# Norming the first two tiles' columns: diagonals behind each root, VectorE instead of GpSimd, and tiles 2 and 3 in a written order

## The chip, the core and the metric

The kernel runs on one core of a Trainium2 chip. A core has TensorE (PE, matrix products into PSUM), VectorE (DVE), ScalarE (ACT), GpSimd (POOL) and SyncE (SP, here only a queue for DMAs). Each engine runs its own instructions in order and waits for others by semaphores. The metric is device time in microseconds (us) of one execution; a smaller time is better.

## What is computed

The kernel is one block of a streaming encoder for 1024 tokens of width 1024, all in float32. Only the first lines of it matter here: the input is normed, and projected by a wide matrix.

```python
def rmsnorm(x, g):
    y = x * lax.rsqrt(jnp.mean(x * x, axis=-1, keepdims=True) + RMS_EPS)
    return y * g

h = rmsnorm(x, norm_mix_pre)                       # 1024 x 1024
proj = jnp.einsum("bsd,dn->bsn", h, w_in)          # q, k, v, f_logit, convolution, gates
...                                                # conv branch, forgetting attention, merge
x = x + rmsnorm(m, norm_mix_post)
x = x + rmsnorm(swiglu(rmsnorm(x, norm_ffn_pre)), norm_ffn_post)
```

## The kernel before

The tokens are cut into eight tiles of 128 rows. For each tile the kernel needs the normed rows transposed (columns of 128 tokens, so that the width lies on the partitions), and it needs them three times over: as a pair of reduced-precision numbers `hB..h` and `hB..l` (high part and rest, made by `split`: ACT copies the high part, DVE subtracts it), and, for the tiles 0 to 3, as full numbers in `hraw`. A product of two such pairs is three passes on PE: high by high (`hh`), high by low (`hl`), low by high (`lh`). The projections that follow use Strassen's scheme, and `hT12` and `hT34` are the sums and differences that it needs. While the columns come in, PE already makes `v` and the forget logits of each tile: `pv`, 8 slices of the width x 3 passes x 2 halves = 48 products a tile, by the weights `wvh` and `wvl`. ACT takes `pv` to `vs`, POOL issues its store to `v_dram`, and DVE adds a bias to the last columns (`ff`).

Tiles 0 and 1 (class `First`) are transposed as they are, before their norm is known: DVE scales the columns by the gain (`hraw`, then the split), the products go ahead, and the token's root (1/norm) is multiplied in when ACT takes `pv` to `vs`. A root is made by `root`: POOL adds epsilon to the sum of squares (`va`) and takes the power -1/2 (`r`). The columns in `hraw` still lack this root, and it differs from column to column. So two diagonal matrices are made from `ident` and the roots, a product with a matrix of ones (`rp`) puts each root in all 128 rows, the columns are multiplied by it, and they are split anew.

Tiles 2 to 7 are normed first: ACT squares and sums (`norm_sum`), POOL makes the root, DVE multiplies (`norm_rest`, which also issues the load of the tile three further on), PE transposes (`turn`, giving `tp`, four banks in turn), and both halves are split. `turn` gives back a function `rest`, called later by hand: for the tiles 2 and 3 it copies `tp` to `hraw`, for the later ones it makes the Strassen sums.

The order: up to the product `rp` all engines keep the order in which the code is written; this is what `steps_` and its row of short names are for (`wh3`: ACT's high part of weight slice 3, `wl1`: DVE's rest of slice 1, `s11`: DVE's scaling of the second half of tile 1, `h11` and `l11`: its split, `x11`: its transposes, `phl01`: PE's pass `hl` of slice 1 for tile 0, `sq` and `pw`: squares and roots). From there on a scheduler decides within a stage where `strict[0]` does not name the engine. Before, tile 2's `rest` was under a written order of DVE, ACT and POOL, and the loop over the tiles from 2 on was free. Every element operation goes through a helper at line 76, so the profile shows one line for all; the names of the tiles tell them apart.

Of the kernel before, what the change touches and what calls it, by code (L numbers as in the profile page):

```python
# [10 lines left out]
F32 = mybir.dt.float32  # L11
F32R = mybir.dt.float32r
AF = mybir.ActivationFunctionType
ALU = mybir.AluOpType
# [3 lines left out]
P = 128  # L18
# [3 lines left out]
ST = S // P  # L22
# [24 lines left out]
def block_kernel(  # L47
# [18 lines left out]
    strict = [()]  # L66

    class InOrder:
# [15 lines left out]
    nc = SimpleNamespace(  # L84
        **{e: InOrder(e) for e in engines}
    )
# [7 lines left out]
    def pool(name, bufs=1, side="left", space=None):  # L94
        kw = dict(name=name, bufs=bufs)
        if space is not DRAM:
            kw["reuse_waits"] = "tile"
        if space is not None:
            kw["space"] = space
        else:  # L100
            kw["side"] = side
        stack = ExitStack()
        ctx.callback(stack.close)
        return stack.enter_context(tc.tile_pool(**kw)), stack.close

    def f32(ap):
        return ap.bitcast(F32)

    def add(o, a, b):
        nc.vector.tensor_tensor(o, a, b, op=ALU.add)  # L110

    def sub(o, a, b):
        nc.vector.tensor_tensor(o, a, b, op=ALU.subtract)

    def mul(o, a, b):
        nc.vector.tensor_tensor(o, a, b, op=ALU.mult)

    def copy(o, a):
        nc.scalar.activation(o, a, AF.Copy)

    def split(hi, lo, src):

        copy(hi, src)
        sub(lo, src, f32(hi))
# [32 lines left out]
    ident = cpool.tile([P, P], F32, name="ident")  # L157
# [19 lines left out]
    def st_tile(name, w=1):  # L177
        return stat.tile([P, w], F32, tag=name, name=name)

    def rms_scale(ms, plus=EPS, tile_=st_tile, w=1, between=None):  # L180

        va = ms
        if plus is not None:
            va = tile_("va", w)
            nc.gpsimd.tensor_scalar(va, ms, plus, None, op0=ALU.add)
        r1 = tile_("r1", w)
        nc.gpsimd.tensor_tensor(r1, va, power[:, :w], op=ALU.pow)
        if between:
            between()
        return r1  # L190
# [7 lines left out]
    def z_tile(name, dt=F32, w=S):  # L198
        return zp.tile([P, S], dt, tag="z", name=name, bufs=2)[:, :w]

    h_pool, h_close = pool("h1", side="right")
    def h_pair(name, shape):
        return [h_pool.tile(shape, F32R, name=f"{name}{t}") for t in "hl"]

    hB11 = h_pair("hB11", [P, 4, NC])
    hT12 = h_pair("hT12", [P, 2, 4, NC])
    hB21 = h_pair("hB21", [P, 4, NC])
# [4 lines left out]
    av, av_close = pool("av")  # L212
    psa, psa_close = pool("psa", 4, space=PSUM)

    def load_x(st, between=None):
        xt = ax.tile([P, D], F32, tag="x", name="xt", bufs=3)
        rows = x2d[st * P : (st + 1) * P, :]
        for c in (n1, n2) if between else (slice(0, D),):
            nc.sync.dma_start(xt[:, c], rows[:, c])
            if between and c is n1:  # L220
                between()
        return xt
# [31 lines left out]
    def vs_tile():  # L254
        return av.tile([P, VF], F32, tag="vs", name="vs", bufs=2)
# [5 lines left out]
    def flat_(t):  # L261
        return t.rearrange("p a b -> p (a b)")
# [22 lines left out]
    def norm_sum(st):  # L285

        xt = xq.pop(st)
        hn = ap.tile([P, D], F32, tag="hn", name="hn", bufs=2)
        ssq = st_tile("ssq")
        nc.scalar.activation(hn, xt, AF.Square, scale=ROOT, accum_out=ssq)  # L290
        return xt, hn, ssq

    def norm_rest(st, xt, hn, rs):

        nc.vector.scalar_tensor_tensor(hn, xt, rs, gm, op0=ALU.mult, op1=ALU.mult)
        if st + 3 < ST:
            xq[st + 3] = load_x(st + 3)
        return hn
# [5 lines left out]
    def turned(hn, q):  # L304

        tp = psa.tile([P, 4, P], F32, tag="mm", name="tp")
        for k in range(4):
            kt = 4 * q + k
            nc.tensor.transpose(tp[:, k, :], hn[:, kt * P : (kt + 1) * P], ident)
        return tp  # L310

    hraw = av.tile([P, KT, NC], F32, name="hraw")

    class First:
# [10 lines left out]
        def turn(self, q):  # L325
            self.tps[q] = turned(self.xt, q)
# [17 lines left out]
        def root(self):  # L344
            self.rs = rms_scale(self.ssq)
# [59 lines left out]
    def v_tile(st, ops):  # L405
        pv = psa.tile([P, 2, NC], F32, tag="pv", name="pv", bufs=2)
        for k in range(KT):
            src = ops[k // 4]
            for n in range(2):
                cs = slice(n * hv, (n + 1) * hv)  # L410
                mm3(
                    pv[:, n, :hv],
                    (src[0][:, k % 4, :], src[1][:, k % 4, :]),
                    (wvh[:, k, cs], wvl[:, k, cs]),
                    k == 0,
                    k == KT - 1,
                )
        v_out(st, pv)
# [3 lines left out]
    def v_out(st, pv, **kw):  # L422
        vs = vs_tile()
        nc.scalar.activation(
            vs.rearrange("p (n c) -> p n c", n=2), pv[:, :, :hv], AF.Copy, **kw
        )
        nc.gpsimd.dma_start(v_dram[st * P : (st + 1) * P, :], vs[:, :AW])
        flast.append((st, vs))
        if st:
            for t, x in flast:  # L430
                add(ff[:, t, :], x[:, AW:VF], bf)
            flast.clear()


    firsts = [First(t) for t in range(2)]
    later, norms = {}, {}

    def square(t):
        if t < 2:
# [8 lines left out]

    def root(t):
        if t < 2:  # L450
            firsts[t].root()
            if t == 0:
                nc.gpsimd.dma_start(bf, b_f[0].partition_broadcast(P))
        else:
            norms[t] = rms_scale(later[t][2])
# [13 lines left out]
    def steps_(row):  # L469
# [7 lines left out]
    parts = [Parts(f.ops) for f in firsts]  # L477
    steps_(
# [5 lines left out]
    )  # L484
    hn = norm_rest(2, *later[2][:2], norms[2])
    steps_("plh06 pw3 phh16 plh16 phl05 phl15 phh07")
    hn3 = norm_rest(3, *later[3][:2], norms[3])
    steps_("pw1")
    cur = turn(2, hn)
    hn = hn3  # L490
    steps_("plh07 phl06 phl07")
    v_out(0, parts[0].pv, scale=firsts[0].rs)
    steps_("phh17 plh17 phl16 phl17")
    v_out(1, parts[1].pv, scale=firsts[1].rs)
    z = z_tile("rs")
    dg = z[:, : 2 * P].rearrange("p (t c) -> p t c", t=2)
    rb = z[:, 2 * P : 4 * P]
    for t, f in enumerate(firsts):
        nc.gpsimd.tensor_scalar(dg[:, t, :], ident, f.rs, None, op0=ALU.mult)
    rp = psa.tile([P, 4, P], F32, tag="mm", name="rp")[:, :2, :]  # L500
    nc.tensor.matmul(flat_(rp), ones, flat_(dg), start=True, stop=True)
    copy(rb, flat_(rp))
    both = slice(0, 2 * P)

    def raw_both(q):
        return hraw[:, 4 * q : 4 * q + 4, both]

    for q in range(2):
        nc.gpsimd.tensor_tensor(
            raw_both(q), raw_both(q), rb.unsqueeze(1).broadcast_to([P, 4, 2 * P]),  # L510
            op=ALU.mult,
        )
    strict[0] = ("vector", "scalar", "gpsimd")
    cur[1]()

    def settle():

        for q, (hh, hl) in enumerate((hB11, hB21)):
            split(hh[:, :, both], hl[:, :, both], raw_both(q))

    strict[0] = ()
    for st in range(2, ST):
        ops, rest = cur
        if st + 1 < ST:
            cur = turn(st + 1, hn)
        if st + 2 < ST:
            hn = norm(st + 2)
        if st + 3 == ST:
            ax_close()
            w0, w0_close = pool("w0", side="right")  # L530

            def w0_tile(tag, dt=F32R):
                return w0.tile([P, KT, P], dt, tag=tag, name=tag, bufs=1)

            r0, h0, l0 = w0_tile("r0", F32), w0_tile("h0"), w0_tile("l0")
            nc.sync.dma_start(r0, win[:, C_Q : C_Q + P].rearrange("(k p) m -> p k m", p=P))
            split(h0, l0, r0)
        if st > 2:
            v_tile(st, ops)
            rest()  # L540
        else:
            v2 = Parts(ops)
            for q in range(2):
                for what in ("hh", "hl", "lh"):
                    v2.run(what, *range(4 * q, 4 * q + 4))
            v_out(2, v2.pv)
            settle()

    av_close()
    ap_close()  # L550
# [557 lines left out]
    for ij, (kind, j, _, _) in enumerate(jobs):  # L1108
# [4 lines left out]
        if ij < 2:  # L1113
            if ij == 0:
# [6 lines left out]
                firsts = []  # L1121
# [52 lines left out]
        elif kind == "gb":  # L1174
            for m, parts in ((j, (c11, c12)), (j + 1, (c21, c22))):
                zt = zts.pop(m)
                for n in range(2):
# [5 lines left out]
                    for t in (1, 0):  # L1183
                        lag = 2 - t
                        c = slice(0 if n else lag, NC)
# [422 lines left out]
    for n in range(2):  # L1608
        ns = slice(n * NC, (n + 1) * NC)
        for d in range(KT):  # L1610
# [16 lines left out]
            if n == 0 and d < 4:  # L1627
                op, half = (w11, w21)[d // 2], slice(d % 2 * 2, d % 2 * 2 + 2)
# [388 lines left out]
    rest = Pairs([f_src(f) for f in range(NPRE)], prep_rest_alone)  # L2017
    whole = Pairs([f_src(f) for f in range(NPRE, NF)])
    for f in range(NF):
# [25 lines left out]
        if f == NF - 2:  # L2045
            ra, rb = pairs_of(raw_t()), pairs_of(raw_t())
# [262 lines left out]
```

## Time and profile before

| | us |
|---|---|
| three timed runs | 1319.67, 1319.72, 1321.43 (median 1319.72) |
| the profiled execution | 1321.18, of it 1319.30 in the span of the trace |
| PE busy | 1307.6 |
| DVE busy | 920.1 |
| ACT busy | 557.1 |
| POOL busy | 192.9 |

The first 65 us of the span are the stage of the tiles; from 64.75 us on the Strassen products `b` begin. A busy PE need not be at full speed: its clock is granted by a throttle, and the windows of the profile show the granted share.

### The profile page before, as it was taken

To read this page: it belongs to the slowest core of one execution; us is meant where nothing else is said; L and a number is where in the kernel's file an instruction comes from. 1 tells how busy PE (TensorE), PEld (TensorE's weight loads), DVE (VectorE), ACT (ScalarE), POOL (GpSimd) and SP (SyncE) were. 2 spreads that over 40 slices of the span, in tenths; PEclk is the share of its full clock that TensorE was granted. 3 is DMA by queue.
4 is the path that set the end of the run, shared out by engine and by line. 5 is a ranking of instruction groups with operands and counts; after the bars stand their busy time and mean duration, and the time that the engine had idled before them with its cause. 6 is when DMAs were issued, how large, how long until landed. Compare 5 with 4: busy or idle time off the path is not lost.

```text
span 1319.3 us, 17686 instructions
## 1 busy us (share of the span) xinstructions
PE 1307.6 (99%) x6695; PEld 1089.6 (83%) x6695; DVE 920.1 (70%) x1312; ACT 557.1 (42%) x868; POOL 192.9 (15%) x351
## 2 busy tenths in 40 slices
PE   8999999999999999999999999999999999999998
PEld 8988888888888888888888878888888888888886
DVE  6983768776656766676677788866766666677674
ACT  6631323344355766513678432222323234344451
POOL 4111001021112222001223112211001110000001
PEclk9999999999999999999999999999999999999999
DMA  6252423555536544674476565533323337966551
GB/s 224 78 171 88 130 71 104 185 203 188 196 138 201 156 142 161 210 252 138 135 229 227 175 193 197 177 120 104 94 90 112 112 104 271 358 224 191 159 168 64
DMA packets 168533, 215.71 MB, mean 164 GB/s; under 512 B 11496, under 2 KB 113968, under 8 KB 168448
## 3 DMA queue, kind: packets, MB, share of 16 engines
q1 hardware_dynamic: 146480, 141.39, 34.4%
q0 software_dynamic: 21952, 73.19, 15.2%
q8 instruction: 52, 0.85, 0.3%
q14 instruction: 33, 0.27, 0.1%
q10 hardware_dynamic: 16, 0.00, 0.0%
HBM read 153.41 MB, written 61.15 MB: 163 GB/s over the span
## 4 chain that ended last, share of the span: by engine, by line
PE 96%; DVE 2%; ACT 1%; issue 1%; DMA 0%; POOL 0%; DVEq 0%; POOLq 0%; ACTq 0%
PE b L76 60%; PE pd L76 16%; PE pba L76 3%; PE pbb L76 3%; PE pv L76 3%; PE po L76 2%; PE tps L76 2%; PE sp L76 2%; PE tp L76 1%; PE ma L76 1%; PE mb L76 1%; DMA raw<-in_w_gate_up_dram 0%; DVE um L76 0%; DVE c L76 0%; PE spin L76 0%
## 5 line engine op out<-in xcount | busy, mean ns | idle before, releaser
L76 DVE TENSOR_TENSOR c<-c,b 128x512 f32<-128x512 f32 x215 | 146.9, 683 | 97.5 <-PE b L76 87.5
L76 DVE TENSOR_TENSOR lo<-raw,hi 128x1024 fp32r<-128x1024 f32 (+1 forms) x91 | 109.7, 1205 | 79.7 <-PE b L76 65.6
L76 ACT ACTIVATE hi<-raw 128x1024 fp32r<-128x1024 f32 (+1 forms) x98 | 99.6, 1016 | 101.9 <-PE b L76 67.9
L76 ACT ACTIVATE hi<-sx 128x1024 fp32r<-128x1024 f32 x44 | 46.8, 1063 | 208.6 <-PE b L76 181.8
L76 DVE TENSOR_TENSOR lo<-sx,hi 128x1024 fp32r<-128x1024 f32 x44 | 53.8, 1223 | 39.2 <-PE b L76 35.8
L76 PE MATMUL b<-w12h,lo 128*128 128x512 f32 x208 | 81.0, 389 | 0.0
L76 PE MATMUL b<-w12l,hi 128*128 128x512 f32 x204 | 79.5, 390 | 0.0
L76 PE MATMUL b<-w12h,hi 128*128 128x512 f32 x204 | 79.5, 390 | 0.0
L76 PE MATMUL b<-hh,hi 128*128 128x512 f32 x176 | 69.1, 393 | 0.4 <-DVE c L76 0.4
L76 PE MATMUL b<-hl,hi 128*128 128x512 f32 x176 | 68.6, 390 | 0.0
L76 PE MATMUL b<-hh,lo 128*128 128x512 f32 x176 | 68.6, 390 | 0.0
L76 DVE TENSOR_TENSOR sx<-raw 128x512 f32<-128x512 f32 x78 | 53.7, 688 | 20.6 <-DMA raw<-in_w_in_dram 11.6
L76 PE MATMUL b<-w,s4h 128*128 128x512 f32 x208 | 64.1, 390 | 0.0
L76 PE MATMUL pd<-hi,lo 128*128 128x512 f32 x160 | 62.4, 390 | 0.0
L76 PE MATMUL pd<-hi 128*128 128x512 f32 x160 | 62.0, 390 | 0.0
L76 POOL DMA_DIRECT2D a_dramA<-um x33 | 17.9, 541 | 276.9 <-DVE um L76 276.3
L76 PE MATMUL pd<-ghi 128*128 128x512 f32 x148 | 57.7, 390 | 0.0
L76 PE MATMUL pd<-glo,ghi 128*128 128x512 f32 x148 | 57.7, 390 | 0.0
L76 PE MATMUL pd<-ghi,glo 128*128 128x512 f32 x148 | 57.6, 390 | 0.0
L76 PE MATMUL b<-hT34h,hi 128*128 128x512 f32 x136 | 53.1, 390 | 0.4 <-DVE c L76 0.4
L76 PE MATMUL b<-hT34h,lo 128*128 128x512 f32 x136 | 53.0, 390 | 0.0
L76 PE MATMUL b<-hT34l,hi 128*128 128x512 f32 x136 | 53.0, 390 | 0.0
(458 smaller groups left out, 3586.7 us busy)
## 6 DMA issues: line engine op xcount, KB each, us to landing
raw<-in_w_gate_up_dram SPq DMA_DIRECT2D x52, 512.0 KB, 3.8
raw<-in_w_in_dram SPq DMA_DIRECT2D x35, 512.0 KB, 3.9
a_dramS<-um POOLq DMA_DIRECT2D x44, 256.0 KB, 3.1
a_dramA<-um POOLq DMA_DIRECT2D x33, 256.0 KB, 2.6
sg<-sg_dram SPq DMA_DIRECT2D x32, 256.0 KB, 4.6
graw<-a_dramS SPq DMA_DIRECT2D x14, 512.0 KB, 4.3
sg_dram<-c POOLq DMA_DIRECT2D x24, 256.0 KB, 2.6
raw<-in_w_down_dram SPq DMA_DIRECT2D x11, 512.0 KB, 4.6
```

The lines of the kernel that those rows point to most:

```text
L76: ins = getattr(self.engine, name)(*args, **kw)
```

## The change

The two diagonals get a tile of their own (`dg`), and each is made on POOL directly behind its root. The product `rp` is put between the passes of tile 2. Its result is no longer copied to SBUF by ACT and multiplied by POOL: DVE multiplies `hraw` by it straight out of PSUM. Tile 2 and the turn of tile 3 no longer run in the free loop but in a written order, with the norm of tile 4 and the new splits of the tiles 0 and 1 at given places; the loop starts at tile 3. In the row of the first two tiles `s11` and `wh3` move forward.

```diff
+    dg = av.tile([P, 2, P], F32, name="dg")
 ...
     def root(t):
         if t < 2:
-            firsts[t].root()
+            f = firsts[t]
+            f.root()
+            nc.gpsimd.tensor_scalar(dg[:, t, :], ident, f.rs, None, op0=ALU.mult)
 ...
-        "phh01 wl1 plh01 z1 wh2 phh10 l10 phl10 phh11 phl01 s11 phl11 phh02 wl2 h11 plh02 phh12 "
-        "plh10 wh3 plh11 plh12 wh4 wl3 phh03 plh03 phh13 wh5 l11 plh13 phl02 wh6 phl12 wl4 "
+        "phh01 s11 plh01 z1 wl1 wh2 phh10 l10 phl10 phh11 wh3 phl01 phl11 phh02 wl2 h11 plh02 phh12 "
+        "plh10 plh11 plh12 wh4 wl3 phh03 plh03 phh13 wh5 l11 plh13 phl02 wh6 phl12 wl4 "
 ...
     cur = turn(2, hn)
-    hn = hn3
 ...
     v_out(1, parts[1].pv, scale=firsts[1].rs)
-    z = z_tile("rs")
-    dg = z[:, : 2 * P].rearrange("p (t c) -> p t c", t=2)
-    rb = z[:, 2 * P : 4 * P]
-    for t, f in enumerate(firsts):
-        nc.gpsimd.tensor_scalar(dg[:, t, :], ident, f.rs, None, op0=ALU.mult)
+    cur[1]()
+    LO_, UP_ = range(4), range(4, 8)
+    v2 = Parts(cur[0])
+    v2.run("hh", *LO_)
     rp = psa.tile([P, 4, P], F32, tag="mm", name="rp")[:, :2, :]
     nc.tensor.matmul(flat_(rp), ones, flat_(dg), start=True, stop=True)
-    copy(rb, flat_(rp))
     both = slice(0, 2 * P)
-    for q in range(2):
-        nc.gpsimd.tensor_tensor(
-            raw_both(q), raw_both(q), rb.unsqueeze(1).broadcast_to([P, 4, 2 * P]),
-            op=ALU.mult,
-        )
-    strict[0] = ("vector", "scalar", "gpsimd")
+    raws = [hraw[:, 4 * q : 4 * q + 4, both] for q in range(2)]
+    v2.run("hl", *LO_)
+    for raw in raws:
+        mul(raw, raw, flat_(rp).unsqueeze(1).broadcast_to([P, 4, 2 * P]))
+    sum4 = norm_sum(4)
+    v2.run("lh", *LO_)
+    cur = turn(3, hn3)
+    hn = norm_rest(4, *sum4[:2], rms_scale(sum4[2]))
+    for what in ("hh", "hl", "lh"):
+        v2.run(what, *UP_)
+    for (hh, hl), raw in zip((hB11, hB21), raws):
+        split(hh[:, :, both], hl[:, :, both], raw)
+    v_out(2, v2.pv)
     cur[1]()
     strict[0] = ()
-    for st in range(2, ST):
+    for st in range(3, ST):
         ops, rest = cur
 ...
-        if st > 2:
-            v_tile(st, ops)
-            rest()
-        else:
-            ...            # tile 2: the passes hh, hl, lh by halves, v_out, the splits
+        v_tile(st, ops)
+        rest()
```

The second `cur[1]()` of the new order is the `rest` of tile 3, and the loop, whose first tile is now 3, calls the same function once more.

What this does to the order on PE, from the end of tile 1's passes to those of tile 2 (`pv` with `hB11` and `hB21`; `tp` are the transposes of tile 3):

```order
 L76 MATMUL pv<-wvl,hB21h 128x260 x4
 L76 MATMUL pv<-wvh,hB11h 128x260 x8
+L76 MATMUL rp<-dg,ones 128x256
 L76 MATMUL pv<-wvl,hB11h 128x260 x8
-L76 MATMUL pv<-wvh,hB11l 128x260 x6
-L76 MATMUL rp<-rs,ones 128x256
+L76 MATMUL pv<-wvh,hB11l 128x260 x8
 L76 MATMUL tp<-ident,hn 128x128 x8
-L76 MATMUL pv<-wvh,hB11l 128x260 x2
 L76 MATMUL pv<-wvh,hB21h 128x260 x8
```

The product `rp` moves forward by 14 products, to a place behind the first eight of tile 2. At the same place on ACT (`vs` of the tiles 0 and 1, the square `hn,ssq` of tile 4, the splits of tile 3):

```order
+L76 ACTIVATE vs<-pv,r_278 128x520
+L76 ACTIVATE vs<-pv,r_414 128x520
+L76 ACTIVATE hraw<-tp 128x4x128 x2
 L76 ACTIVATE hn,ssq<-xt 128x1024
-L76 ACTIVATE vs<-pv,r_412 128x520
-L76 ACTIVATE rs<-rp 128x256
-L76 ACTIVATE hraw<-tp 128x4x128 x2
 L76 ACTIVATE hB11h<-tp 128x4x128
 L76 ACTIVATE hB21h<-tp 128x4x128
```

Tile 1's `vs` and the copies of tile 2's columns now stand ahead of tile 4's square, and the copy of `rp` is gone. On DVE, from the biases of tiles 0 and 1 to the scaling of tile 5 (`hn`):

```order
-L76 TENSOR_TENSOR ff<-vs,bf 128x8
-L76 SCALAR_TENSOR_TENSOR hn<-xt,r_479,gm 128x1024
-L76 TENSOR_TENSOR ff<-vs,bf 128x8
+L76 TENSOR_TENSOR ff<-vs,bf 128x8 x2
+L76 TENSOR_TENSOR hraw<-hraw,rp 128x4x256 x2
 L76 TENSOR_TENSOR hB11l<-tp,hB11h 128x4x128
 L76 TENSOR_TENSOR hB21l<-tp,hB21h 128x4x128
+L76 SCALAR_TENSOR_TENSOR hn<-xt,r_503,gm 128x1024
 L76 TENSOR_TENSOR hB11l<-hraw,hB11h 128x4x256
 L76 TENSOR_TENSOR hB21l<-hraw,hB21h 128x4x256
```

The scaling of tile 4 (the first `hn`) moves from ahead of tile 3's splits to behind them, and the two multiplications by `rp` stand ahead of both. On SP the loads of tiles 4 and 5 change places: tile 4's goes out first now and waits for the end of tile 1's square, where before it went out when tile 2 had been scaled.

More of the change, by code (lines that the diff above doesn't have):

```diff
@@ L494, in block_kernel @@
     v_out(1, parts[1].pv, scale=firsts[1].rs)
-    z = z_tile("rs")
-    dg = z[:, : 2 * P].rearrange("p (t c) -> p t c", t=2)
-    rb = z[:, 2 * P : 4 * P]
-    for t, f in enumerate(firsts):
-        nc.gpsimd.tensor_scalar(dg[:, t, :], ident, f.rs, None, op0=ALU.mult)
+    cur[1]()
+    LO_, UP_ = range(4), range(4, 8)
+    v2 = Parts(cur[0])
+    v2.run("hh", *LO_)
     rp = psa.tile([P, 4, P], F32, tag="mm", name="rp")[:, :2, :]
     nc.tensor.matmul(flat_(rp), ones, flat_(dg), start=True, stop=True)
-    copy(rb, flat_(rp))
     both = slice(0, 2 * P)
-    def raw_both(q):
-        return hraw[:, 4 * q : 4 * q + 4, both]
-    for q in range(2):
-        nc.gpsimd.tensor_tensor(
-            raw_both(q), raw_both(q), rb.unsqueeze(1).broadcast_to([P, 4, 2 * P]),
-            op=ALU.mult,
-        )
-    strict[0] = ("vector", "scalar", "gpsimd")
+    raws = [hraw[:, 4 * q : 4 * q + 4, both] for q in range(2)]
[11 more added lines that the diff above has]
+    v_out(2, v2.pv)
     cur[1]()
-    def settle():
-        for q, (hh, hl) in enumerate((hB11, hB21)):
-            split(hh[:, :, both], hl[:, :, both], raw_both(q))
     strict[0] = ()
-    for st in range(2, ST):
+    for st in range(3, ST):
         ops, rest = cur
@@ L537, in block_kernel @@
             split(h0, l0, r0)
-        if st > 2:
-            v_tile(st, ops)
-            rest()
-        else:
[L542 to L547, printed above, removed]
+        v_tile(st, ops)
+        rest()
     av_close()
```

## The prediction

> **What bounds the kernel now.** I read the page first, then the waits of TensorE (PE), then the windows and the timeline around the longest wait. The first line below is the page's row of busy time; the other two are the longest rows of PE's waits (who waited for whom: us in total, times, longest).
>
> ```profile
> PE 1307.6 (99%) x6695; PEld 1089.6 (83%) x6695; DVE 920.1 (70%) x1312; ACT 557.1 (42%) x868; POOL 192.9 (15%) x351
> PE rp L76 <- POOL rs L76: 2.4, 1, 2.4
> PE spin L76 <- DVE zero L76: 1.4, 1, 1.4
> ```
>
> PE is busy for 99% of the span, so the time is PE's work, its clock and its few holes. The largest hole that a semaphore explains is 2.43 us before `rp`, the product that turns the roots of tiles 0 and 1 into columns. The windows around it (length; busy us of PE, PEld, DVE, ACT, POOL; then granted clock, DMA share, GB/s):
>
> ```profile
> 23.89:26.32 2.43, 0.00 (x1) 0.00 (x1) 1.53 (x2) 0.00 (x0) 2.32 (x3) 1.00 0.71 256
> 26.32:27.08 0.76, 0.76 (x5) 0.66 (x6) 0.00 (x0) 0.00 (x0) 0.00 (x0) 1.00 0.87 97
> 27.08:30.49 3.41, 3.41 (x18) 3.14 (x17) 1.29 (x2) 2.84 (x6) 2.91 (x2) 0.50 0.31 126
> ```
>
> The hole has a second bill: 0.76 us after work resumes the granted clock falls to 0.50 and stays there for 3.41 us, in which PE does half the work. The same on PE's timeline (start, us, then the operation):
>
> ```profile
> 18.39 1.03 PE L76 MATMUL tp<-ident,hn 128*128 128x128 f32 x8
> 19.18 0.48 PE L76 MATMUL pv<-wvh,hB21l 128*128 128x260 f32 x2
> ...
> 20.99 1.22 PE L76 MATMUL pv<-wvh,hB11h 128*128 128x260 f32 x8
> 22.05 1.12 PE L76 MATMUL pv<-wvl,hB11h 128*128 128x260 f32 x8
> 23.01 0.88 PE L76 MATMUL pv<-wvh,hB11l 128*128 128x260 f32 x6
> 26.32 0.70 PE L76 MATMUL rp<-rs,ones 128*128 128x256 f32 x2 [2.43 <-POOL rs L76]
> 26.85 1.81 PE L76 MATMUL tp<-ident,hn 128*128 128x128 f32 x8
> 28.90 1.84 PE L76 MATMUL pv<-wvh,hB21h 128*128 128x260 f32 x8
> 30.58 1.12 PE L76 MATMUL pv<-wvl,hB21h 128*128 128x260 f32 x8
> 31.54 1.12 PE L76 MATMUL pv<-wvh,hB21l 128*128 128x260 f32 x8
> 32.50 1.04 PE L76 MATMUL tp<-ident,hn 128*128 128x128 f32 x8
> ```
>
> At full clock eight `pv` products take 0.96 us (22.05 to 23.01, 30.58 to 31.54) and eight transposes 0.79 (18.39 to 19.18); at half clock they took 1.68 (28.90 to 30.58). Why `rp` was late stands on ACT, POOL and SP:
>
> ```profile
> 18.10 7.44 SPq L76 DMA_DIRECT2D xt<-in_x_dram  x4
> 18.46 0.19 ACT L76 ACTIVATION_READ_ACCUMULATOR xt<-xt 128x1 f32 x1
> 19.03 0.60 ACT L76 ACTIVATE hB11h<-tp 128x512 fp32r<-128x512 f32 x1 [0.37 <-PE tp L76]
> 20.27 0.57 POOL L76 TENSOR_TENSOR r<-va,power 128x1 f32<-128x1 f32 x1
> 21.75 1.06 ACT L76 ACTIVATE hn<-xt 128x1024 f32<-128x1024 f32 x1 [0.81 <-DMA xt<-in_x_dram]
> 22.80 0.68 ACT L76 ACTIVATE vs<-pv,r 128x520 f32<-128x520 f32 x1
> 23.83 0.62 POOL L76 DMA_DIRECT2D v_dram<-vs  x1
> L76 POOL TENSOR_SCALAR rs<-ident,r x2: 592/882/1172, 24.5 to 25.7; 128x128 f32<-128x128 f32 x2
> ```
>
> The second root is ready at 20.84 (20.27 + 0.57). But the diagonals stand on POOL behind the store of `vs` of tile 1; that `vs` stood on ACT behind tile 4's square, and the square waited for tile 4's load. So 3.7 us pass between the root and the first diagonal, for no reason of data.
>
> **The change, part by part.**
>
> *Diagonals behind each root.* The second one starts at about 20.9 and takes 0.59 to 1.17 (the two ends of the row above), so it is there between 21.5 and 22.1. PE asks for it after the eight `hh` products, at 22.05. I take 0.59, since the 1.17 ran beside tile 4's scaling on DVE, which is no longer there: no wait; at the other end 0.05. What goes is the hole: six products at 0.12 from 23.01 end their turn at 23.73, the next one started at 26.32, so 2.59 us. And with it the half clock: 3.41 x 0.5 = 1.71. `rp` itself is moved and costs what it did (0.53 from start to start). Counted forward from 20.99 instead: 1.06 for `hh`, 0.45 for `rp`, 0.96 and 0.96 for `hl` and `lh`, 0.79 for tile 3's transposes, 2.88 for the upper 24 products, and PE reaches tile 4's transposes at 28.1 where it was 32.50: 4.4, against 4.3 by the two terms. I take 4.3.
>
> That an idle stretch of 2.43 us brings half clock is this trace's own row. "TensorE: Matmul & The Clock Gate", the Trainium skill's page, in the section "HAM oscillation — how this bites in real kernels", warns only of idle gaps above about 3.4 us; by that the 1.71 would not have been paid and the sum would be 2.59. The row contradicts the threshold. The page's other statement, that the window of 3413 ns runs free, fits the row's 3.41 us, and would let the loss fall on some executions and not on others.
>
> *The columns normed by DVE out of PSUM.* Out go the copy of `rp` on ACT and two POOL multiplications; in come two DVE ones of 1024 elements a row. The trace has none with a PSUM operand of that size:
>
> ```profile
> 23.90 1.28 DVE L76 SCALAR_TENSOR_TENSOR hn<-xt,r,gm 128x1024 f32<-128x1024 f32 x1 [2.52 <-POOL r L76]
> 29.00 0.69 DVE L76 TENSOR_TENSOR hB11l<-tp,hB11h 128x512 fp32r<-128x512 f32 x1 [3.56 <-ACT hB11h L76]
> 31.09 2.31 DVE L76 TENSOR_TENSOR hB11l<-hraw,hB11h 128x1024 fp32r<-128x1024 f32 x1 [0.80 <-ACT hB11h L76]
> 33.43 1.23 DVE L76 TENSOR_TENSOR hB21l<-hraw,hB21h 128x1024 fp32r<-128x1024 f32 x1
> 35.45 1.28 DVE L76 SCALAR_TENSOR_TENSOR hn<-xt,r,gm 128x1024 f32<-128x1024 f32 x1 [0.79 <-ACT b12h L76]
> L76 POOL TENSOR_TENSOR hraw<-hraw,rs x2: 2376/2384/2392, 27.6 to 29.9; 128x1024 f32<-128x1024 f32 x2
> ```
>
> The lower end is 1.23 (same engine and size, 33.43), the upper 2.38 (the same work on POOL). I take 1.25: PSUM as a source cost nothing at 512 elements (0.69 at 29.00, beside a running POOL multiplication). So they run from 22.6 to 25.1, in DVE's present idle time (2.52 and 3.56 us), and are free unless what stands behind them is late. That is tile 3's two splits, then tile 4's scaling `hn`, now behind them, on which PE's tile 4 transposes wait, and with them all of PE.
>
> *That path.* From the start of a tile's transposes the trace has 0.64 to ACT's `hB11h` (18.39 to 19.03), then 0.60 for it; then DVE's two splits at a pitch of 0.61 (29.00 and 29.61), the second at 1.90, and at the same pitch `hn` from 2.50 to 3.78 (1.28). PE's own way from there is 0.79 + 2.88 = 3.67. So PE waits some 0.15 us; 0 if ACT is a little quicker, 1.8 if the multiplications take 2.38 each (DVE free at 27.4, `hn` at 29.9 against 28.1). I take 0.15. Tile 4's root is early enough: its load now goes out after tile 1's square (18.65) instead of 18.10 and lands, at the 3.65 us that it took, at 22.3, while ACT comes to it at 22.8 (after `vs` at about 21.15 and two copies of `hraw`); the root follows at 24.9, and `hn` asks at 26.9.
>
> *The reordered row of tiles 0 and 1.* PE's sequence is the same; on DVE tile 1's second scaling (0.6) goes ahead of `wvl` of slice 1, which PE reads at 10.47:
>
> ```profile
> 9.15 0.69 DVE L76 TENSOR_TENSOR wvl<-wr,wvh 128x520 fp32r<-128x520 f32 x1
> 10.47 0.64 PE L76 MATMUL pv<-wvl,hB11h 128*128 128x260 f32 x4
> ```
>
> It ends at 10.44 then, still 0.03 ahead, or 0.1 to 0.2 late where the first diagonal on POOL holds DVE up (the 2.31 at 31.09 against 1.23 shows that such a hold exists). I take 0.05. The stretch from 10 to 20 us has no PE hole, so the earlier `wvh` gains nothing.
>
> *A second copy.* The new order calls the rest of tile 3 once by hand and once in the loop: two more ACT copies of 512, 1.08 us a pair (27.39 below), on a half idle engine. They stand ahead of tile 6's square, whose `hn` PE needs some 6 us later: 0.
>
> Sum: -2.59 - 1.71 + 0.15 + 0.05 = -4.1, from the profiled 1321.18 (span 1319.30 and 1.88 around it) to 1317.1. The three timed runs are 1319.67, 1319.72 and 1321.43. Their two groups lie 1.7 apart, the profiled one in the upper, and 1.7 is just the half clock's price. I read it so: the median run has the hole but not the half clock, and only 2.59 - 0.2 = 2.4 to win: 1317.3. Between both: **1317.2**, with 1316.6 to 1317.7 as its own range. This is 2.5 us or 0.19% under the median; 0.2% (2.64 us, 1317.08) is about what a measurement of this kernel can tell from no change, so the most likely result lies on that edge.
>
> **Rivals.**
>
> 1. *The timed runs all pay the half clock* and their spread is something else. Then the median wins the whole 4.1: 1315.6. For it: one profiled execution shows it. Against: the 1.7 between the groups. Chance 0.20.
>
> 2. *The wait moves to tile 4's `hn`.* With multiplications of 1.8 to 2.38, PE waits 0.6 to 1.8: 1317.8 to 1319.0; a wait of 1.8 might also bring the half clock, 1320.7. All of it stays within 0.2% of the median. Against: the DVE rows of 1024 shown here take 1.23 to 1.28 except the one that POOL held, and POOL's long work is gone. Chance 0.13.
>
> 3. *Slower: DVE becomes the bound in tiles 4 to 7.* From 36 to 66.4 us it is busy 28.82 of 30.40:
>
> ```profile
> 36.00:66.40 30.40, 30.40 (x252) 30.12 (x251) 28.82 (x41) 20.29 (x31) 4.94 (x10) 1.00 0.28 88
> 27.39 1.08 ACT L76 ACTIVATE hraw<-tp 128x512 f32<-128x512 f32 x2
> 56.71 0.68 DVE L76 TENSOR_TENSOR b12l<-tp,b12h 128x512 fp32r<-128x512 f32 x1
> 59.24 0.28 PE L76 MATMUL pv<-wvh,b12l 128*128 128x260 f32 x1
> ```
>
> Tile 7's split is done at 57.4 and read at 59.24: 1.84 us in hand. If DVE is not earlier at all, PE, 4.1 earlier, waits 2.3 and the time is 1319.4. If the two multiplications (2.5) and the second copy (1.08) come on top, the split is done at 61.0 and all is later than now: 1321.18 + 1.74 = 1322.9, slower. It decides from DVE 3.0 us later than now (1322.36). Against: DVE idles 2.52 + 3.56 + 0.80 + 0.79 us between 21 and 36, and the 1.09 that POOL held it in the 2.31 go too; I make `hn` of tile 5 at 31 instead of 35.45, as early as PE. Chance 0.05 for slower, 0.04 for the 1319.4.
>
> **How the numbers follow.** The forecast has 0.58, of which four tenths (0.23) lie under 1317.08; rival 1 0.20; rival 2 0.13; rival 3 0.09. Faster: 0.23 + 0.20 = 0.43. Same: 0.35 + 0.13 + 0.04 = 0.52. Slower: 0.05. The range goes from under rival 1 to the top of rival 2 without half clock: 1315.2 to 1319.1.
>
> **What the changed profile would show.** Right: no wait of PE for POOL; `rp` at about 22; granted clock 1.00 from 22 to 34; DVE's multiplications near 1.25 each; tile 4's transposes at 28.1 to 28.4; `b` from 60.5 instead of 64.75. Wrong: a PE wait for `hn` near 28 of 0.5 or more (rival 2); PE waits for DVE at 34 to 60 (rival 3); the hole gone and the timed gain 4 (rival 1). If its profiled execution, without half clock, again lies 1.5 us above its timed runs, my reading of the two groups is wrong.

## The result, and the profile after

The changed kernel takes 1317.50 us (median of 13 runs, 1316.56 to 1319.51) where the kernel before takes 1321.11 (13 runs beside them, 1319.67 to 1324.13): a ratio of 0.9973, with a 95% interval of 0.9965 to 0.9982. It is 3.6 us, or 0.27%, faster. Three runs had shown 1319.72 as the median of before; ten more put it at 1321.11.

PE's longest waits in the changed kernel (the same view as before's):

```profile
PE spin L76 <- DVE zero L76: 1.4, 1, 1.4
PE b L76 <- DVE c L76: 0.6, 2, 0.4
PE po L76 <- ACT ptT L76: 0.3, 1, 0.3
PE tp L76 <- ACT raw L76: 0.3, 1, 0.3
...
PE pv L76 <- DVE wvl L76: 0.2, 1, 0.2
```

The 2.4 us that `rp` waited for POOL are gone; the wait for `wvl` in the last line is new. PE's timeline from tile 2's transposes to tile 4's:

```profile
18.99 1.03 PE L76 MATMUL tp<-ident,hn 128*128 128x128 f32 x8
...
21.59 1.23 PE L76 MATMUL pv<-wvh,hB11h 128*128 128x260 f32 x8
22.65 0.60 PE L76 MATMUL rp<-dg,ones 128*128 128x256 f32 x2
22.89 1.31 PE L76 MATMUL pv<-wvl,hB11h 128*128 128x260 f32 x8
24.04 1.13 PE L76 MATMUL pv<-wvh,hB11l 128*128 128x260 f32 x8
25.00 1.04 PE L76 MATMUL tp<-ident,hn 128*128 128x128 f32 x8
25.80 1.20 PE L76 MATMUL pv<-wvh,hB21h 128*128 128x260 f32 x8
26.84 1.12 PE L76 MATMUL pv<-wvl,hB21h 128*128 128x260 f32 x8
27.80 1.12 PE L76 MATMUL pv<-wvh,hB21l 128*128 128x260 f32 x8
28.90 1.06 PE L76 MATMUL tp<-ident,hn 128*128 128x128 f32 x8
```

From one set of transposes to the other it is 28.90 - 18.99 = 9.91 us, where it was 32.50 - 18.39 = 14.11: 4.20 us less. This stretch is the yardstick for all that follows, because it holds all that the change moves on PE's path, but for the wait for `wvl`, and nothing of the start. The windows from `rp` to tile 4's transposes and of the two stretches behind (columns as before's: busy time of each engine, granted clock, DMA share, GB/s):

```profile
22.65:28.90 6.25, 6.25 (x52) 6.04 (x51) 5.02 (x7) 5.10 (x9) 1.32 (x3) 1.00 0.38 153
28.90:35.57 6.67, 6.67 (x58) 6.67 (x57) 5.15 (x7) 5.69 (x12) 3.02 (x5) 1.00 0.38 123
35.57:61.33 25.76, 25.76 (x219) 25.76 (x218) 23.84 (x36) 15.99 (x23) 3.92 (x6) 1.00 0.21 63
```

PE is busy throughout and its clock stays at 1.00. What feeds it, from the timelines of POOL, ACT and DVE:

```profile
9.05 1.15 POOL L76 TENSOR_SCALAR dg<-ident,r 128x128 f32<-128x128 f32 x1
20.43 0.62 POOL L76 TENSOR_SCALAR dg<-ident,r 128x128 f32<-128x128 f32 x1
21.79 0.69 ACT L76 ACTIVATE vs<-pv,r 128x520 f32<-128x520 f32 x1 [0.26 <-PE pv L76]
23.28 2.35 DVE L76 TENSOR_TENSOR hraw<-hraw,rp 128x1024 f32<-128x1024 f32 x2 [0.59 <-PE rp L76]
27.48 1.28 DVE L76 SCALAR_TENSOR_TENSOR hn<-xt,r,gm 128x1024 f32<-128x1024 f32 x1
```

The second diagonal is ready at 21.05, 1.6 us before PE comes to `rp`. The two multiplications take 2.35 together. Tile 4's `hn` ends at 28.76, just when PE comes to its transposes (27.80 + 0.96 = 28.76), and they start 0.14 later.

The two profiled executions differ by less than the yardstick: 1321.18 and 1318.41, that is 2.77. The changed one came to tile 2 0.60 later (18.99 against 18.39), and lost 0.70 more near 697 us, at the transposes that wait for `raw` (from tile 4's transposes to the products behind these it took 670.09 instead of 669.39). The second profile of it, below, came to tile 2 at 18.75, has no such loss near 697 us, and ends at 1316.91.

### The profile page after: what moved, and what is told of

Read it like the earlier page. It is cut to its first block, busy times and chain, and to the rows that moved or that the text cites. A ratio compares the mean times of both kernels' runs of the same rounds, so it can differ in the third digit from the quotient of the medians.

```text
span 1316.5 us, 17693 instructions
## 1 busy us (share of the span) xinstructions
PE 1307.0 (99%) x6695; PEld 1088.9 (83%) x6695; DVE 920.7 (70%) x1314; ACT 557.3 (42%) x869; POOL 189.8 (14%) x349
## 4 chain that ended last, share of the span: by engine, by line
PE 95%; DVE 2%; ACT 1%; DMA 1%; issue 1%; POOL 0%; DVEq 0%; POOLq 0%; ACTq 0%; SPq 0%
PE b L76 59%; PE pd L76 16%; PE pv L76 3%; PE pba L76 3%; PE pbb L76 3%; PE po L76 2%; PE tps L76 2%; PE sp L76 2%; PE tp L76 1%; PE ma L76 1%; DMA raw<-in_w_gate_up_dram 1%; PE mb L76 1%; DVE um L76 0%; DVE c L76 0%; PE spin L76 0%
## 5 line engine op out<-in xcount | busy, mean ns | idle before, releaser
L76 PE MATMUL b<-hT12h,lo 128*128 128x512 f32 x136 | 53.0, 390 | 0.0
```

Of the source, the lines that this page charges most:

```text
L76: ins = getattr(self.engine, name)(*args, **kw)
```

## The experiments

Rows that name the same median of before share these runs of before. "Yardstick" is the time from tile 2's to tile 4's transposes on PE in the kernel's profiled execution; before 14.11, changed kernel 9.91.

| kernel | yardstick | median, runs | before beside it, runs | ratio, 95% interval |
|---|---|---|---|---|
| changed | 9.91 | 1317.50, 13 | 1321.11, 13 | 0.9973, 0.9965 to 0.9982 |
| before, early diagonals | 12.18 | 1319.53, 11 | 1321.29, 33 | 0.9989, 0.9980 to 0.9998 |
| the same, with DVE's multiplications | 11.00 | 1318.19, 9 | 1321.05, 13 | 0.9977, 0.9967 to 0.9987 |
| changed, late diagonals | 12.00 | 1319.96, 11 | 1321.29, 33 | 0.9994, 0.9984 to 1.0003 |
| before, hole filled | 12.85 | 1320.54, 11 | 1321.29, 33 | 0.9991, 0.9982 to 1.0000 |
| changed, POOL's multiplications | 12.01 | 1321.01, 11 | 1321.29, 33 | 0.9998, 0.9989 to 1.0007 |
| changed, again | 9.91 | 1317.63, 9 | 1321.40, 14 | 0.9976, 0.9966 to 0.9986 |
| changed, trimmed | 9.92 | 1317.23, 5 | 1321.40, 14 | 0.9967, 0.9954 to 0.9979 |
| trimmed, tile 4 scaled earlier | 9.76 | 1317.66, 6 | 1321.40, 14 | 0.9968, 0.9957 to 0.9979 |
| before, again | 14.13 | 1322.12, 1 | | |

**Only the diagonals, early** (kernel before).

```diff
+    dg = av.tile([P, 2, P], F32, name="dg")
 ...
-            firsts[t].root()
+            f = firsts[t]
+            f.root()
+            nc.gpsimd.tensor_scalar(dg[:, t, :], ident, f.rs, None, op0=ALU.mult)
 ...
-    dg = z[:, : 2 * P].rearrange("p (t c) -> p t c", t=2)
 ...
-    for t, f in enumerate(firsts):
-        nc.gpsimd.tensor_scalar(dg[:, t, :], ident, f.rs, None, op0=ALU.mult)
```

> The kernel before, with only the two diagonals moved directly behind their roots; GpSimd still multiplies, the loop over the tiles is as before. The scheduler then puts rp ahead of tile 2's first products. Measure: from the start of tile 2's transposes on TensorE to the start of tile 4's, 14.11 us before, 9.91 in the changed kernel. Theory (the late diagonal is the loss, the rest of the change only keeps new waits small): TensorE waits about 0.5 us for the second diagonal at its new earlier place and about 1.0 us for a bank that ScalarE still has to copy, the clock stays at 1.00, 11.2 us from transposes to transposes, time 2.5 to 3.0 us under before. Rival (the diagonals alone do all of it): below 10.3 us, time as the changed kernel. Rival (without VectorE's multiplications nothing is won): 13 us or more.

The yardstick is 12.18: the hole and the half clock are gone, but 1 us more was lost than expected, and the time is 1.8 us under before where 2.5 to 3.0 were expected. PE's timeline:

```profile
21.43 0.70 PE L76 MATMUL rp<-dg,ones 128*128 128x256 f32 x2 [0.25 <-POOL dg L76]
23.99 0.66 PE L76 MATMUL tp<-ident,hn 128*128 128x128 f32 x4 [0.59 <-ACT rs L76]
30.65 1.06 PE L76 MATMUL tp<-ident,hn 128*128 128x128 f32 x8 [1.07 <-DVE ff L76]
```

DVE's and POOL's:

```profile
24.08 6.42 DVE L76 SCALAR_TENSOR_TENSOR hn<-xt,r,gm 128x1024 f32<-128x1024 f32 x1 [2.59 <-POOL r L76]
30.43 0.15 DVE L76 TENSOR_TENSOR ff<-vs,bf 128x8 f32<-128x8 f32 x1
24.68 4.74 POOL L76 TENSOR_TENSOR hraw<-hraw,rs 128x1024 f32<-128x1024 f32 x2
```

The third line of PE names `ff`, but what it waited for is `hn`, whose 1.28 us became 6.42: it ended 1.08 after POOL's two multiplications (29.42). With early diagonals these multiplications come at the very time at which DVE scales tile 4, and both read SBUF. In the kernel before, the late diagonal had put them behind that scaling; there another DVE instruction was held in the same way (the 2.31 at 31.09 where 1.23 is usual), and it too ended 1.09 after POOL's second multiplication (32.31). The expectation had not seen it. The Trainium skill names a cause: in "SBUF — State Buffer", section "Who interferes with whom", a DVE instruction with two inputs in SBUF contends with a GpSimd instruction that reads SBUF, because they share a read port. That fits the end of `hn`. The section's remark that the order of issue decides who blocks does not show in the records, in which `hn` starts 0.60 before POOL's first multiplication and yet ends behind both.

**The same, with DVE's multiplications.** This was run last, to test that reading.

```diff
-    copy(rb, flat_(rp))
 ...
-        nc.gpsimd.tensor_tensor(
-            raw_both(q), raw_both(q), rb.unsqueeze(1).broadcast_to([P, 4, 2 * P]),
-            op=ALU.mult,
-        )
+        mul(raw_both(q), raw_both(q), flat_(rp).unsqueeze(1).broadcast_to([P, 4, 2 * P]))
```

> The kernel before with the early diagonals and with VectorE's multiplications out of PSUM, but without the written order of tiles 2 and 3: the first experiment plus one edit. Theory (the first experiment lost its second half because GpSimd's multiplications held VectorE in tile 4's scaling for 5.1 us): the scaling takes 1.28 again, the wait of 1.07 us at tile 4's transposes goes, the 0.25 for the diagonal and about 0.5 for the bank stay: 10.7 us from tile 2's to tile 4's transposes, of the 9.91 of the whole change; the rest is the written order's. Rival (the wait came from elsewhere, as the profile's name for its releaser says): 11.5 us or more.

Its timelines of DVE (two lines) and PE:

```profile
24.99 1.28 DVE L76 SCALAR_TENSOR_TENSOR hn<-xt,r,gm 128x1024 f32<-128x1024 f32 x1 [2.72 <-POOL r L76]
26.27 2.34 DVE L76 TENSOR_TENSOR hraw<-hraw,rp 128x1024 f32<-128x1024 f32 x2
22.50 0.70 PE L76 MATMUL rp<-dg,ones 128*128 128x256 f32 x2 [0.50 <-POOL dg L76]
25.11 0.65 PE L76 MATMUL tp<-ident,hn 128*128 128x128 f32 x4 [0.39 <-ACT hraw L76]
30.29 1.03 PE L76 MATMUL tp<-ident,hn 128*128 128x128 f32 x8
```

`hn` takes 1.28 again and PE no longer waits at tile 4's transposes, so the loss did come from POOL's multiplications; that the port is the reason is the skill's account and not shown here. The yardstick is 11.00 (expected 10.7; the wait for the diagonal was 0.50 and not 0.25). So the three parts of the change are worth, one upon the other, 1.93 us (diagonals), 1.18 (multiplications) and 1.09 (written order), 4.20 together. The medians go the same way: 1.8, 2.9 and 3.6 to 3.8 under before.

**The changed kernel with late diagonals.**

```diff
-            nc.gpsimd.tensor_scalar(dg[:, t, :], ident, f.rs, None, op0=ALU.mult)
 ...
     v_out(1, parts[1].pv, scale=firsts[1].rs)
+    for t, f in enumerate(firsts):
+        nc.gpsimd.tensor_scalar(dg[:, t, :], ident, f.rs, None, op0=ALU.mult)
```

> The changed kernel, with only the two diagonals put back behind both stores of vs on GpSimd. Theory: rp waits for them again, some 1.9 us (stores issued until 23.3, two diagonals until 24.5, rp asked for at 22.65), all that follows is as much later, and if the clock falls to 0.50 for 3.4 us another 1.7: 11.8 us from tile 2's to tile 4's transposes without, 13.5 with the fall. Rival (the written order and VectorE's multiplications win the time): it stays within 0.5 us of the changed kernel's 9.91.

Its timeline of PE:

```profile
18.78 1.03 PE L76 MATMUL tp<-ident,hn 128*128 128x128 f32 x8
24.43 0.70 PE L76 MATMUL rp<-dg,ones 128*128 128x256 f32 x2 [1.83 <-POOL dg L76]
30.78 1.06 PE L76 MATMUL tp<-ident,hn 128*128 128x128 f32 x8
```

The window behind the hole (columns as above):

```profile
24.43:30.78 6.35, 6.35 (x50) 6.14 (x51) 4.98 (x6) 3.26 (x5) 0.79 (x2) 1.00 0.27 112
```

A hole of 1.83 is back, and the yardstick is longer by a little more than that (12.00, 2.09 more). The granted clock stays at 1.00 behind it.

**The hole filled** (kernel before; the products of zeros go to a bank that `rp` overwrites; tile 2's first 22 products are written ahead of them, where the scheduler had put them anyway).

```diff
+    v2 = Parts(cur[0])
+    v2.run("hh", *range(4))
+    v2.run("hl", *range(4))
+    v2.run("lh", *range(3))
+    for _ in range(22):
+        nc.tensor.matmul(flat_(rp), zero[:, 0, :], flat_(zero[:, :2, :]), start=True, stop=True)
     nc.tensor.matmul(flat_(rp), ones, flat_(dg), start=True, stop=True)
 ...
-            v2 = Parts(ops)
-            for q in range(2):
-                for what in ("hh", "hl", "lh"):
-                    v2.run(what, *range(4 * q, 4 * q + 4))
+            v2.run("lh", 3)
+            for what in ("hh", "hl", "lh"):
+                v2.run(what, *range(4, 8))
```

> The kernel before, with 22 products of zeros (128x256, 0.114 us each) in the hole ahead of rp, which nothing reads: it leaves every wait and the real work as they were and takes away only the idle time that the clock gate sees. Theory: the granted clock stays at 1.00, rp starts when it did, and tile 2's to tile 4's transposes take 12.4 us instead of 14.11. If all timed runs of before pay for the half clock, the timed gain is 1.7 us; by the prediction's reading of the three times (the median run has the hole but not the half clock) it is under 0.5. Rival (the clock falls for another reason than the idle time): 0.50 again, 14.1 us.

Its timeline of PE, with the added products in the second line:

```profile
20.42 1.03 PE L76 MATMUL tp<-ident,hn 128*128 128x128 f32 x8
25.76 2.79 PE L76 MATMUL rp<-zero 128*128 128x256 f32 x22
28.41 0.70 PE L76 MATMUL rp<-rs,ones 128*128 128x256 f32 x2
28.95 1.35 PE L76 MATMUL tp<-ident,hn 128*128 128x128 f32 x8
30.06 0.49 PE L76 MATMUL pv<-wvh,hB11l 128*128 128x260 f32 x2
...
33.27 1.03 PE L76 MATMUL tp<-ident,hn 128*128 128x128 f32 x8
```

The window behind `rp`:

```profile
28.41:31.80 3.39, 3.29 (x26) 2.95 (x25) 0.70 (x2) 2.34 (x5) 2.12 (x1) 1.00 0.49 147
```

`rp` starts 7.99 after tile 2's transposes, as before (26.32 - 18.39 = 7.93), and the clock behind it is 1.00, as the theory had it. By itself this profile does not show that the filling did it, because of when the clock can change. In the traces' records of the clock each stretch from one change to the next is a whole multiple of 3.413 us: in the kernel before 20.48 at 1.00 (six of them), 3.41 at 0.50 (one), 1286.83 at 1.00 (377). The clock thus changes only at edges that lie 3.413 apart, and what went with a fall is how long PE was busy between two edges. Three such stretches, of the kernel before, of the changed kernel with POOL's multiplications (below) and of the changed kernel with late diagonals:

```profile
23.67:27.08 3.41, 0.98 (x7) 0.67 (x7) 1.53 (x2) 0.00 (x0) 2.54 (x4) 1.00 0.77 232
27.15:30.57 3.42, 1.36 (x12) 1.17 (x11) 1.42 (x3) 2.49 (x5) 1.99 (x4) 1.00 0.00 0
20.77:24.18 3.41, 1.82 (x14) 1.51 (x13) 0.89 (x3) 3.15 (x6) 2.19 (x4) 1.00 0.92 333
```

PE was busy for 0.29, 0.40 and 0.53 of them (roughly, since the ends of its products are modelled); behind the first two the clock fell to 0.50, behind the third it did not. The eleven profiles hold fourteen falls (three behind holes, and one at the end of each kernel, where PE's work is over): each stands behind a stretch with a share of 0.40 or less, and no stretch with 0.53 or more, from the clock's first rise on, has one behind it. So idle time does go with the fall, but its place counts as well as its length. In the filled kernel an edge lies at 26.95. Without the products of zeros PE would have been idle there from 25.92 to 28.41, 1.03 ahead of the edge and 1.46 behind it, which leaves shares of 0.70 and 0.57: by the same count its clock would have stayed at 1.00 in any case.

The yardstick is 12.85, 0.45 more than expected. Of it 0.32 are tile 3's transposes (1.11 from start to start, 0.79 elsewhere), which stand beside ACT's copies of `rp` and of tile 2's columns (29.21 to 30.57) and probably wait for them. In time the filled kernel is 0.75 us under before, with an interval from 0 to 2.4: more than nothing at the edge of what can be told, and no proof that every run pays.

**Before once more.**

> The kernel before once more, for a second look at its hole. Theory: the hole of 2.4 us and the half clock behind it are the rule and not an accident of the one profiled execution: 14.1 us from tile 2's to tile 4's transposes. By the prediction's reading of the three times about two executions in three would show the hole without the half clock, 12.4 to 12.9 us.

Its timeline of PE:

```profile
18.46 1.03 PE L76 MATMUL tp<-ident,hn 128*128 128x128 f32 x8
26.39 0.70 PE L76 MATMUL rp<-rs,ones 128*128 128x256 f32 x2 [2.43 <-POOL rs L76]
```

A window behind the hole:

```profile
28.00:30.00 2.00, 2.00 (x11) 2.00 (x10) 0.93 (x2) 1.53 (x4) 2.00 (x2) 0.50 0.07 29
```

The same hole to the hundredth and the same half clock; tile 4's transposes begin at 32.59, a yardstick of 14.13.

**The changed kernel with POOL's multiplications.**

```diff
-        mul(raw, raw, flat_(rp).unsqueeze(1).broadcast_to([P, 4, 2 * P]))
+    rb = z_tile("rs")[:, : 2 * P]
+    copy(rb, flat_(rp))
+        nc.gpsimd.tensor_tensor(raw, raw, rb.unsqueeze(1).broadcast_to([P, 4, 2 * P]), op=ALU.mult)
```

> The changed kernel, with the columns multiplied as before: rp copied to SBUF by ScalarE, two multiplications on GpSimd. Theory: rp is as early as in the changed kernel, but the multiplications (2.38 us each) stand on GpSimd ahead of tile 4's root, which is ready at about 29.4 instead of 25.5; TensorE waits for tile 4's hn about 1.9 us and tile 2's to tile 4's transposes take 11.8 us, 13.5 if the clock falls too. Rival (where the multiplication runs is of no account): 9.9 us, no wait, time as the changed kernel.

Its timelines of POOL (two lines), DVE and PE:

```profile
23.41 4.75 POOL L76 TENSOR_TENSOR hraw<-hraw,rs 128x1024 f32<-128x1024 f32 x2 [0.50 <-ACT rs L76]
28.55 0.57 POOL L76 TENSOR_TENSOR r<-va,power 128x1 f32<-128x1 f32 x1
29.16 1.28 DVE L76 SCALAR_TENSOR_TENSOR hn<-xt,r,gm 128x1024 f32<-128x1024 f32 x1 [2.00 <-POOL r L76]
30.59 1.94 PE L76 MATMUL tp<-ident,hn 128*128 128x128 f32 x8 [2.08 <-DVE hn L76]
```

The window behind PE's wait:

```profile
31.00:33.80 2.80, 2.80 (x15) 2.80 (x14) 2.42 (x4) 2.54 (x6) 2.64 (x3) 0.50 0.65 193
```

As expected: tile 4's root waits behind the multiplications, PE waits 2.08 us for `hn`, and the clock falls to 0.50 behind that. The yardstick of 12.01 does not hold the half clock, which lies behind tile 4's transposes; with it (1.7) the trace leaves about 0.4 of the 4.2, and in time nearly the whole gain is gone (1321.01 against 1321.29). PE's wait is the one of the prediction's second rival, brought about by hand, though here tile 4's root on POOL is late and not DVE's multiplications.

**Trimmed, and tile 4 scaled earlier.** The first takes out the second copy of tile 3's columns (the last line shown) and the new row of the tiles 0 and 1; the second also moves `turn` behind `norm_rest`. The changed kernel itself ran beside them.

```diff
-    cur = turn(3, hn3)
     hn = norm_rest(4, *sum4[:2], rms_scale(sum4[2]))
+    cur = turn(3, hn3)
 ...
     v_out(2, v2.pv)
-    cur[1]()
```

> The changed kernel without the second copy of tile 3's columns and with the old row of tiles 0 and 1 (wvl of slice 1 ahead of s11 on VectorE, h11 ahead of wh3 on ScalarE). Theory: both edits are off TensorE's path but for the 0.15 us that it waited for wvl at 10.8; that wait goes, and in time nothing that can be measured (0 to 0.2 us). Rival (the second copy delays tile 6's scaling enough to be felt, or the new row wins time): 0.5 us or more away from the changed kernel.

> As the trimmed kernel, and VectorE scales tile 4 ahead of tile 3's two splits, in the 0.64 us in which it idled after its multiplications. Theory: the wait of 0.14 us at tile 4's transposes goes, 9.75 us from tile 2's to tile 4's transposes; the splits end about 0.6 us later, still ahead of tile 3's products. Rival: the splits come too late and TensorE waits for them instead.

> The changed kernel once more, beside the trimmed ones and on their chip. Theory: no wait for GpSimd, 9.9 to 10.0 us from tile 2's to tile 4's transposes, a time 3 to 4 us under before. It also shows how far the early part (to tile 2's transposes at 18.99 in the first profile, 18.39 in before's) varies from execution to execution with the same code: theory, 0.3 us or more either way.

No wait for `wvl` is listed in either, nor in the second profile of the changed kernel, where `wvl` ended at 10.67 and PE read it at 10.72; in the trimmed kernels it was ready 0.4 to 0.5 ahead. The yardsticks are 9.92 and 9.76, and in the second of them tile 4's `hn` is scaled where DVE idled (25.22, against 27.48 in the changed kernel). Its timelines of DVE and PE:

```profile
25.22 1.28 DVE L76 SCALAR_TENSOR_TENSOR hn<-xt,r,gm 128x1024 f32<-128x1024 f32 x1
28.42 1.03 PE L76 MATMUL tp<-ident,hn 128*128 128x128 f32 x8
```

So the 0.15 us at tile 4's transposes can be won in the profile. In time the three kernels beside each other cannot be told apart (1317.63, 1317.23, 1317.66): neither the second copy nor the row of the first tiles is worth anything that these runs can tell, and no version was found that is measurably better than the change.

## Why the prediction was right, point by point

- *The hole (-2.59) and the half clock (-1.71), with 0.15 and 0.05 of new waits: -4.1.* The yardstick shrank by 4.20 (the 0.05 lies ahead of it, so 4.15 were forecast for it). Each price was read from the profile: the diagonal took 0.62 (0.59 taken), the multiplications 1.18 each (1.25 taken), `hn` ended 0.14 before PE's start on tile 4's transposes (a wait of 0.15 taken), `rp` started 1.06 after tile 2's first products. Tile 4's transposes began at 28.90 and `b` at 61.17, where 28.1 to 28.4 and 60.5 were forecast; the 0.60 by which this execution came later to tile 2 is the difference. That the late diagonal made the hole is shown by putting it back (a hole of 1.83).
- *`wvl` of slice 1 (0.05 taken, up to 0.2).* The wait was 0.15. But the reason given for it did not occur: POOL's first diagonal ran from 9.05 to 10.20, and the DVE instructions beside it took their usual 0.68 to 0.69, so it held nothing up. `wvl` began at 10.22, straight behind `s11`, which had itself come later than reckoned.
- *The second copy: nothing.* So it is.
- *DVE in the tiles 4 to 7 (rival 3).* PE waited for DVE nowhere between 29 and 61 us; PE was busy for all of the 25.76 us from 35.57 to 61.33.
- *The step that failed: the reading of the three times.* I took 1319.7 and 1321.4 for two groups, executions without and with the half clock, and so gave the median only 2.4 us to win. The 13 runs of the result and the 33 of the first experiments lie between 1319.2 and 1324.4 without a gap that would part them into two groups, a second profile of before has the same hole and the same half clock, and the medians are 1321.1 to 1321.4. Four comparisons (the change twice, and the two trimmed kernels) gave 3.6 to 4.2 where I had allowed 2.4. The first profiled execution was an ordinary one and two of the three timed runs were quick ones. What spreads the runs is elsewhere: tile 2's transposes began between 18.39 and 20.42 in eleven profiles of nearly the same code, the two latest after a wait of 0.65 to 0.70 for a load of `x`; in these two the clock's record reaches 1.00 only at 9.88 and 10.16, in the others between 6.25 and 7.92. So the absolute time (1317.2 against 1317.5) came out by luck: the start was put 1.4 too low and the gain 1.1 too low, and the two errors cancel. The gain was put at 0.19% where it is 0.27%, and the larger chance stood on "within 0.2%". Rival 1 (all runs pay; 4.1 us to win) was nearer than the 0.20 that it got. The prediction's own sign of this error stayed silent: the profiled execution lay 0.9 above the median of its timed runs, not 1.5.
- *What stays open.* The median gained 3.6 to 3.8, the yardstick 4.2; for the filled hole it is 0.75 and 1.26, for the late diagonal 1.33 and 2.11. The differences lie within the intervals, for the late diagonal at the very end of its own. If some executions of before escape the half clock, the medians would fall short in this way, and the edges give a way to escape. My estimate: I set the hole of before, 5.50 to 7.93 behind tile 2's transposes, among the edges of all eleven profiles. In nine of them it lies wholly or nearly so between two edges (share 0.35 or less); in two, those that came to tile 2 latest, it would be split and leave 0.59 or more. But both profiles of before pay, and no timed run shows whether any escapes.

## What to carry to other kernels

When an engine keeps its written order, look at what stands between a value being ready and its use: here a diagonal had all its data 3.7 us before it was begun, behind a store that waited for another engine's load. Moving it forward moved the next piece of work into a neighbour's way, and the whole gain needed the multiplication on another engine too: try the parts one by one before crediting one of them. And a few runs are no distribution: three times that seem to fall into two groups say nothing of two states.

## What the runs showed of the hardware

- The granted clock changed only at edges 3.413 us apart. It fell to 0.50, for one such stretch of 3.41 us, where PE had been busy for 0.29 (twice, holes of 2.43 us) and 0.40 (a hole of 2.08) of the stretch before; it stayed at 1.00 behind shares of 0.53 and more (a hole of 1.83 that reached over an edge; three of 0.25, 0.59 and 1.07). The limit lies between 0.40 and 0.53 of a stretch, and a hole's length alone does not tell. The Trainium skill's "TensorE: Matmul & The Clock Gate", section "HAM oscillation — how this bites in real kernels", warns of idle gaps above about 3.4 us; here 2.08 was enough.
- A multiplication on POOL can stretch a DVE instruction beside it from 1.28 to 6.42 us, through two POOL instructions without a gap for DVE between them. A DVE instruction that read PSUM for one of its inputs was not slowed beside the same work: the split of 512 elements at 25.86 took 0.69 while POOL multiplied from 23.41 to 28.16 (changed kernel with POOL's multiplications).
- A wait that has several sources is not always named rightly: the 1.07 us put down to `ff` were those of `hn` ahead of it.
